# Layer 0 of a two-layer attention trunk: the rotation summed in PSUM, the heads' combination moved from VectorE to GpSimd

## The chip, the core and the metric

The kernel runs on one core of a Trainium2 chip. The metric is the device time of one execution in microseconds (us). The engines are named as the profile names them: PE is TensorE (matmuls; PEld its weight loads), DVE is VectorE, ACT is ScalarE, POOL is GpSimd, SP is SyncE, which issues the DMAs here. Each engine takes its own instructions in the order in which they stand; semaphores let one wait for another. SBUF is the memory that all of them work in; PSUM holds the results of matmuls, in eight banks of 128 partitions x 512 float32. The time before is a median of 2046.3 us over three runs (2044.1 to 2049.32).

## The reference

Two layers over 1024 tokens of width 1024, each a normalisation, a mixer and a residual. Layer 0 mixes with dilated window attention: 16 heads of 64, each in three groups with (window, dilation) = (128, 1), (512, 4), (2048, 16), so 48 attentions, whose results are combined by their softmax denominators and gated. Cut to what matters here:

```python
def dilated_mixer(h, w_in, w_out):
    proj = h @ w_in
    q = rope(qkv[:, :, 0], pos)          # x1*cos - x2*sin, x2*cos + x1*sin
    k = rope(qkv[:, :, 1], pos)
    v = qkv[:, :, 2]
    for g, (window, dil) in enumerate(DIL_GROUPS):
        o, lse = dilated_window_attention(q[:, :, sl], k[:, :, sl], v[:, :, sl], window, dil)
        ...
    alpha = jax.nn.softmax(jnp.stack(lses, axis=0), axis=0)
    o = jnp.sum(alpha[..., None] * jnp.stack(outs, axis=0), axis=0)
    y = o.reshape(B, S, DIL_WIDTH) * jax.nn.silu(gate)
    return y @ w_out
```

Layer 1 is a differential attention of eight heads. All of it is float32. The kernel splits each matrix operand into a high part that the matmul takes whole and a low part (the rest), and adds three products, so that a float32 product costs three matmuls.

## The kernel before, in words

The transposed, normalised input stays in SBUF as `XH` (high) and `XL` (low). First come the values of layer 0 and most of its gates. Then two strands run interwoven on PE. One is the attention: 8 pairs of heads x 3 groups x 2 heads, each head in four steps `c` of two blocks of 128 queries: `scores` (with the masked minimum on DVE at L583 and the exponential on ACT at L586), three steps later `transposes` (PE at L599; ACT casts the high part `pp`, L603, and DVE subtracts it from PSUM to get the low part, L122), and five steps later `product` with the values. The other strand, the filler, makes the rotated queries and keys in 24 units, one for a pair and a group (`qk_unit`).

A unit loads two weight blocks of 128 x 1024 (`raw`), splits each into `wh` (ACT, L184) and `wl` (`low`, L122), and runs for each half of the tokens (512) two projections of 24 matmuls, one for each half of the head dimension, into two PSUM tiles `pp[0]` and `pp[1]`. Both have the tag `pj` of the pool `ps`. That pool has four tags of two buffers of one bank (`pj`, `s`, `pt`, `u`), so that the next projection takes the bank of `pp[0]` again. On the engines, the tiles of the projections are called `pqk`. The rotation (L247 to L252) makes four products on DVE from `pp` and the tables into SBUF tiles `t`, and the difference and the sum on POOL into `r`; in groups 1 and 2 the output of these is put in the order of the residues (`put`, strided). Then `r` is split again (ACT L256, `low` alternating between DVE and POOL by `alt()`) and stored to DRAM, from which the heads load it.

`product` ends with the sum of the high and the low half of the values, into `u`: for groups 0 and 1 in `store` (L654 on ACT copies one half from PSUM to the single buffer `ul`, L659 on DVE adds), for group 2 in `alone` (L645 and L647 on ACT, L646 and L649 on DVE, the last one from SBUF to SBUF, strided). When the third group of a pair has its scores, `put_stats` and `joint` send the softmax statistics through DRAM (`st_d` to `js`, some small operations on DVE from L691 on, then `wt_d`), and after its last product `combine` loads the weights as `wb`, multiplies the three `u` (L715), adds them (L720), multiplies with the gate (L721), and `put_y` splits and stores the result.

PE's order is written out by hand: it is the order of the program. A filler step is taken wherever `fill.at` is called, three times in each step of the attention, up to a goal that grows by four matmuls a call; before the attention it runs 2.4 units ahead (`LEAD0`). The order on the other engines is chosen by a scheduler when the program is built.

Of the kernel before, what the change touches and what calls it, by code (L numbers as in the profile page):

```python
# [10 lines left out]
F32 = mybir.dt.float32  # L11
F32R = mybir.dt.float32r
# [80 lines left out]
def trunk(ctx: ExitStack, tc: tile.TileContext, a: dict, out: bass.AP):  # L93
# [126 lines left out]
    def qk_unit(pool, unit, w, sub=1, on_pool=False):  # L220

        tiles = []
        for half in range(2):
            wh, wl = w_tiles([P, KT, P])
            split(wh, wl, load(w[half], [P, KT, P]))
            tiles.append((wh, wl))
        r = [pool.tile([P, T], F32, tag="r", name="r", bufs=3 - on_pool) for _ in range(2)]
        for c in range(2):
            tok = ts(c, 512)
            pp = []  # L230
            for half in range(2):
                o = ps.tile([P, 512], F32, tag="pj", name="pqk")
                yield from project(o, *tiles[half], tok)
                pp.append(o)
            nat = (lambda t: t) if sub == 1 else (lambda t: t.rearrange("p (a r) -> p a r", r=sub))
            put = lambda t: t.rearrange("p (r c a) -> p c a r", r=sub, c=2)[:, c]
            if sub == 1:
                put = lambda t: t[:, tok]
            x, eng = pp, nc.vector
            if on_pool:  # L240
                x, eng = [pool.tile([P, 512], F32, tag="x", name="x") for _ in range(2)], nc.gpsimd
                for i in range(2):
                    nc.scalar.copy(x[i], pp[i])
            t1, t2, t3, t4 = (
                pool.tile([P, 512], F32, tag="t", name="t", bufs=3 - on_pool) if i < 2 or not on_pool
                else x[i - 2] for i in range(4))
            eng.tensor_mul(t1, x[0], cos[:, tok])  # L247
            eng.tensor_mul(t3, x[0], sin[:, tok])
            eng.tensor_mul(t2, x[1], sin[:, tok])  # L249
            nc.gpsimd.tensor_sub(put(r[0]), nat(t1), nat(t2))  # L250
            eng.tensor_mul(t4, x[1], cos[:, tok])  # L251
            nc.gpsimd.tensor_add(put(r[1]), nat(t4), nat(t3))  # L252
        written.add(unit)
        for e in range(2):
            rh = pool.tile([P, T], F32R, tag="rh", name="rh")
            nc.scalar.copy(rh, r[e])  # L256
            low(nc.vector if on_pool else alt(), r[e].bitcast(F32R), r[e], rh)
            for i, t in enumerate((rh.bitcast(F32), r[e])):
                nc.sync.dma_start(qk_d[unit, :, :, i, e].rearrange("s h f t -> f (s h) t"), t)
# [99 lines left out]
    def put_y(layer, kt, c, y, hi):  # L359
# [7 lines left out]
        nc.scalar.copy(hi, y)  # L367
        low(nc.vector, y.bitcast(F32R), y, hi)
# [160 lines left out]
    with tc.tile_pool(name="l0", bufs=2) as lp, early0 as ep:  # L529
# [4 lines left out]
        class Head:  # L534
# [99 lines left out]
            def alone(self, c):  # L634
# [14 lines left out]
                nc.vector.tensor_add(by_residue(uo, SUB[2])[:, 2 * c : 2 * c + 2, :], us_[:HD], ul)  # L649
# [56 lines left out]
        def combine(pr, us):  # L706
            fill.until(("gate", 0, pr))
            for c in range(2):
                tok = ts(c, 512)
                for g in range(NG):  # L710
# [4 lines left out]
                    (nc.vector if pr == 7 else alt()).tensor_mul(us[g][:, tok], us[g][:, tok], wb)  # L715
                sil = lp.tile([P, 512], F32, tag="sil_in", name="sil_in", bufs=1)
                nc.sync.dma_start(sil, sil_d[0][pr, :, tok])
                y = us[0][:, tok]
                for g in (1, 2):
                    (nc.vector if pr == 7 else nc.gpsimd).tensor_add(y, y, us[g][:, tok])  # L720
                nc.vector.tensor_mul(y, y, sil)  # L721
                put_y(0, pr, c, y, us[1][:, tok])
# [20 lines left out]
        for i in range(nst + LAG_P):  # L743
            if i < nst:
                hd, c = heads[i // 4], i % 4
                if c == 0 and hd.h == 0:
                    stats[hd.pr, hd.g] = lp.tile([P, 2, 2, NB], F32, tag="st", name="st")
                    us[hd.pr, hd.g] = lp.tile([P, T], F32, tag="u", name="u", bufs=3)
# [322 lines left out]
```

## Time and profile before

| | us |
|---|---|
| median of three runs | 2046.3 |
| the profiled execution, its own time | 2049.16 |
| its span, first to last instruction | 2047.3 |
| PE busy (share of the span) | 1911.4 (93%) |
| DVE busy | 1145.4 (56%) |
| ACT busy | 886.6 (43%) |
| POOL busy | 617.5 (30%) |

The profile is of one execution. In its groups, a row gives line, engine, operation and tiles (output<-inputs), their number, the busy time, the mean of one in ns, and after the bar the idle time of the engine just before and what ended it. A row of the timeline gives start, duration, engine, line, operation, and in brackets the idle time before and what ended it. Lines named L122, L184 are in the helpers `low` and `split` and serve many places; the tile names tell which. Matmuls overlap, so the duration of one is longer than the distance to the next. A row of the windows gives, for a stretch, the busy time of each engine (number of instructions), the granted share of the TensorE clock, the DMA engines' busy share and GB/s.

### The profile page before, as it was taken

To read this page: it belongs to the slowest core of one execution; us is meant where nothing else is said; L and a number is where in the kernel's file an instruction comes from. 1 tells how busy PE (TensorE), PEld (TensorE's weight loads), DVE (VectorE), ACT (ScalarE), POOL (GpSimd) and SP (SyncE) were. 2 spreads that over 40 slices of the span, in tenths; PEclk is the share of its full clock that TensorE was granted. 3 is DMA by queue.
4 is the path that set the end of the run, shared out by engine and by line. 5 is a ranking of instruction groups with operands and counts; after the bars stand their busy time and mean duration, and the time that the engine had idled before them with its cause. 6 is when DMAs were issued, how large, how long until landed. Compare 5 with 4: busy or idle time off the path is not lost.

```text
span 2047.3 us, 28864 instructions
## 1 busy us (share of the span) xinstructions
PE 1911.4 (93%) x10008; PEld 1598.6 (78%) x10008; DVE 1145.4 (56%) x2771; ACT 886.6 (43%) x2055; POOL 617.5 (30%) x386
## 2 busy tenths in 40 slices
PE   6999999999999999999999969899999899999888
PEld 4788888888787787788787848688879788887776
DVE  3311122146776767676767655570066877777626
ACT  3312122135555555555555555341245455546522
POOL 2000000143443434353535330230561534433121
PEclk8999999999999999999999979899999999999999
DMA  5424244277696969696969697542446565555643
GB/s 207 145 93 138 99 146 161 102 222 231 198 298 192 296 190 304 182 301 191 299 197 297 195 328 227 183 172 97 142 154 190 165 196 162 195 183 177 239 155 124
DMA packets 218018, 397.90 MB, mean 194 GB/s; under 512 B 40976, under 2 KB 123408, under 8 KB 217872
## 3 DMA queue, kind: packets, MB, share of 16 engines
q1 hardware_dynamic: 217872, 396.04, 60.7%
q8 instruction: 80, 1.31, 0.3%
q14 instruction: 66, 0.54, 0.1%
HBM read 254.87 MB, written 132.71 MB: 189 GB/s over the span
## 4 chain that ended last, share of the span: by engine, by line
PE 67%; DVE 11%; DMA 10%; ACT 4%; POOL 3%; issue 3%; SPq 1%; POOLq 0%; DVEq 0%; ACTq 0%
PE pqk L275 25%; PE pv L213 16%; PE pg L275 7%; PE po L377 3%; PE sc L576 3%; DMA wb<-wt_d 2%; PE sc L894 2%; PE up L626 2%; PE pe L420 2%; PE tp L599 2%; PE ob L945 2%; DVE u L649 1%; DMA st_d<-st 1%; POOL r L252 1%; DVE pm L897 1%
## 5 line engine op out<-in xcount | busy, mean ns | idle before, releaser
L275 PE MATMUL pqk<-XL,wh 128*128 128x512 f32 x1024 | 423.1, 413 | 0.0
L275 PE MATMUL pqk<-XH,wl 128*128 128x512 f32 x1024 | 411.8, 402 | 0.0
L275 PE MATMUL pqk<-XH,wh 128*128 128x512 f32 x1024 | 410.7, 401 | 0.9 <-DVE t L251 0.9
L122 POOL TENSOR_TENSOR wl<-raw,wh 128x1024 fp32r<-128x1024 f32 x41 | 98.5, 2402 | 612.1 <-ACT wh L184 612.1
L586 ACT ACTIVATE pm<-pm,st 128x128 f32<-128x128 f32 (+1 forms) x384 | 170.2, 444 | 155.9 <-DVE st L583 154.0
L275 PEld LDWEIGHTS pqk<-XH,wh 128*128 128x128 f32 x1024 | 194.9, 190 | 30.4 <-DVE t L251 1.9
L275 PEld LDWEIGHTS pqk<-XL,wh 128*128 128x128 f32 x1024 | 195.3, 191 | 27.6
L275 PEld LDWEIGHTS pqk<-XH,wl 128*128 128x128 f32 x1024 | 195.6, 191 | 27.2
L213 PE MATMUL pv<-vwh,XH 128*128 128x512 f32 (+1 forms) x448 | 173.8, 388 | 8.3 <-ACT XH L158 4.6
L250 POOL TENSOR_TENSOR r<-t 128x512 f32<-128x512 f32 x64 | 98.1, 1533 | 270.2 <-DVE t L249 269.2
L213 PE MATMUL pv<-vwl,XH 128*128 128x512 f32 (+1 forms) x448 | 172.4, 385 | 2.8 <-POOL vwl L122 2.8
L213 PE MATMUL pv<-vwh,XL 128*128 128x512 f32 (+1 forms) x448 | 172.6, 385 | 1.4 <-DVE XL L122 0.8
L184 ACT CAST wh<-raw 128x1024 fp32r<-128x1024 f32 x98 | 102.5, 1047 | 151.6 <-PE pqk L275 73.3
L122 DVE TENSOR_TENSOR wl<-raw,wh 128x1024 fp32r<-128x1024 f32 x57 | 76.0, 1333 | 147.6 <-ACT wh L184 147.3
L122 DVE TENSOR_TENSOR vs<-pv,vs 128x512 fp32r<-128x512 f32 x64 | 44.1, 689 | 200.5 <-ACT vs L495 187.9
L904 ACT ACTIVATE pm<-pm,mx 128x256 f32<-128x256 f32 (+7 forms) x128 | 99.4, 777 | 123.2 <-DVE mx L903 64.8
L122 DVE TENSOR_TENSOR pp<-tp,pp 128x512 fp32r<-128x512 f32 (+2 forms) x192 | 104.0, 541 | 80.8 <-ACT pp L603 79.2
L599 PE MATMUL tp<-ident,pm 128*128 128x128 f32 x560 | 96.3, 281 | 39.8 <-DVE pp L122 39.5
L599 PEld LDWEIGHTS tp<-ident,pm 128*128 128x128 f32 x560 | 73.1, 144 | 73.1 <-issue 36.5
L583 DVE CUSTOM_DVE_ANT_0 pm<-sc,masks 128x128 f32<-128x128 f32 (+1 forms) x384 | 118.7, 343 | 17.1 <-PE sc L576 15.7
L897 DVE CUSTOM_DVE_ANT_0 pm<-sc,md 128x512 f32<-128x512 f32 (+3 forms) x192 | 102.7, 551 | 31.1 <-PE sc L894 28.6
L495 ACT CAST vs<-pv 128x512 fp32r<-128x512 f32 x48 | 28.1, 586 | 187.2 <-PE pv L213 187.2
(516 smaller groups left out, 4441.0 us busy)
## 6 DMA issues: line engine op xcount, KB each, us to landing
qk_d<-rh SPq DMA_DIRECT2D x64, 512.0 KB
qk_d<-r SPq DMA_DIRECT2D x64, 512.0 KB
qh<-qk_d SPq DMA_DIRECT2D x128, 256.0 KB
ql<-qk_d SPq DMA_DIRECT2D x128, 256.0 KB
ka<-qk_d SPq DMA_DIRECT2D x64, 512.0 KB
v_d<-vs SPq DMA_DIRECT2D x48, 512.0 KB
raw<-in_dil_qk_dram SPq DMA_DIRECT2D x48, 512.0 KB
vt<-v_d SPq DMA_DIRECT2D x48, 512.0 KB
```

The lines of the kernel that those rows point to most:

```text
L122: eng.tensor_tensor(o, full, hi.bitcast(F32), ALU.subtract)
L184: nc.scalar.copy(wh, raw)
L213: nc.tensor.matmul(o, lhsT=l, rhs=r_, start=first and k == 0, stop=last and k == 3 * KT - 1, skip_group_check=True)
L250: nc.gpsimd.tensor_sub(put(r[0]), nat(t1), nat(t2))
L275: nc.tensor.matmul(o, lhsT=l[:, kt, :], rhs=r_[:, kt, tok], start=k == 0, stop=k == 3 * KT - 1)
L377: nc.tensor.matmul(banks[c], lhsT=l[:, kt, ts(n)], rhs=r_[:, ts(c, 512)], start=first and k == 0, stop=last and k == 2,)
L576: nc.tensor.matmul(sc[:, cols], lhsT=q[:, ts(b)], rhs=kv, start=k == 0, stop=k == 1)
L583: nc.vector.tensor_tensor_reduce(pm[:, cols], sc[:, cols], m[:, m.shape[1] - w_ :], 1.0, 3.0e38, ALU.add, ALU.min, st[:, 0, j : j + 1])
L586: nc.scalar.activation(pm[:, cols], pm[:, cols], AF.Exp, bias=st[:, 0, j : j + 1], scale=-1.0, accum_out=st[:, 1, j : j + 1])
L599: nc.tensor.transpose(out=tp[:, ts(n)], in_=self.pb.pop((b, kb)), identity=ident)
L897: nc.vector.tensor_tensor_reduce(pm[:, k0:k1], sc[:, :w_], m_, 1.0, 3.0e38, ALU.add, ALU.min, mx[:, j : j + 1])
L904: nc.scalar.activation(pm[:, :wq], pm[:, :wq], AF.Exp, bias=mx[:, 0:1], scale=-1.0, accum_out=den)
```

## The change

- `qk_unit` in layer 0 makes the whole rotation on DVE. The product of `pp[1]` and the sines is written into `pp[0]`, the product of `pp[1]` and the cosines into `pp[1]` itself, and the difference and the sum are taken by DVE, each from one SBUF tile and one PSUM tile. The four `t` tiles become two.
- Both weight splits and both low parts of `r` are done by POOL (before, half of them).
- In `alone`, the last sum (from `us_` and `ul` into `u`) is done by POOL.
- `combine` runs on POOL for the pairs 0 to 6 (for pair 7 on DVE, as before), in the group order 0, 2, 1, with each sum right after its product; the gate and the high and low parts of `put_y` are done by the same engine. The gate's tile shares the three buffers of `wb`. `u` has four buffers, not three.

Layer 1 keeps its rotation on POOL.

```diff
@@ def qk_unit
-            split(wh, wl, load(w[half], [P, KT, P]))
+            split(wh, wl, load(w[half], [P, KT, P]), None if on_pool else nc.gpsimd)
...
-            t1, t2, t3, t4 = (
-                pool.tile([P, 512], F32, tag="t", name="t", bufs=3 - on_pool) if i < 2 or not on_pool
-                else x[i - 2] for i in range(4))
-            eng.tensor_mul(t1, x[0], cos[:, tok])
-            eng.tensor_mul(t3, x[0], sin[:, tok])
-            eng.tensor_mul(t2, x[1], sin[:, tok])
-            nc.gpsimd.tensor_sub(put(r[0]), nat(t1), nat(t2))
-            eng.tensor_mul(t4, x[1], cos[:, tok])
-            nc.gpsimd.tensor_add(put(r[1]), nat(t4), nat(t3))
...
+                t1, t2 = (pool.tile([P, 512], F32, tag="t", name="t") for _ in range(2))
+                nc.vector.tensor_mul(t1, pp[0], cos[:, tok])
+                nc.vector.tensor_mul(t2, pp[0], sin[:, tok])
+                nc.vector.tensor_mul(pp[0], pp[1], sin[:, tok])
+                nc.vector.tensor_sub(put(r[0]), nat(t1), nat(pp[0]))
+                nc.vector.tensor_mul(pp[1], pp[1], cos[:, tok])
+                nc.vector.tensor_add(put(r[1]), nat(pp[1]), nat(t2))
...
-            low(nc.vector if on_pool else alt(), r[e].bitcast(F32R), r[e], rh)
+            low(nc.vector if on_pool else nc.gpsimd, r[e].bitcast(F32R), r[e], rh)
@@ def put_y(layer, kt, c, y, hi, eng=None)
-        nc.scalar.copy(hi, y)
-        low(nc.vector, y.bitcast(F32R), y, hi)
+        if eng is None:
+            nc.scalar.copy(hi, y)
+        else:
+            eng.tensor_copy(hi, y)
+        low(eng or nc.vector, y.bitcast(F32R), y, hi)
@@ def alone
-                nc.vector.tensor_add(by_residue(uo, SUB[2])[:, 2 * c : 2 * c + 2, :], us_[:HD], ul)
+                nc.gpsimd.tensor_add(by_residue(uo, SUB[2])[:, 2 * c : 2 * c + 2, :], us_[:HD], ul)
@@ def combine
+            eng = nc.vector if pr == 7 else nc.gpsimd
             for c in range(2):
                 tok = ts(c, 512)
-                for g in range(NG):
+                y = us[2][:, tok]
+                for g in (0, 2, 1):
...
-                    (nc.vector if pr == 7 else alt()).tensor_mul(us[g][:, tok], us[g][:, tok], wb)
-                sil = lp.tile([P, 512], F32, tag="sil_in", name="sil_in", bufs=1)
+                    eng.tensor_mul(us[g][:, tok], us[g][:, tok], wb)
+                    if g:
+                        eng.tensor_add(y, y, us[1 if g == 1 else 0][:, tok])
+                sil = lp.tile([P, 512], F32, tag="wb", name="sil_in", bufs=3)
                 nc.sync.dma_start(sil, sil_d[0][pr, :, tok])
-                y = us[0][:, tok]
-                for g in (1, 2):
-                    (nc.vector if pr == 7 else nc.gpsimd).tensor_add(y, y, us[g][:, tok])
-                nc.vector.tensor_mul(y, y, sil)
-                put_y(0, pr, c, y, us[1][:, tok])
+                eng.tensor_mul(y, y, sil)
+                put_y(0, pr, c, y, us[1][:, tok], eng)
@@ the loop of layer 0
-                    us[hd.pr, hd.g] = lp.tile([P, T], F32, tag="u", name="u", bufs=3)
+                    us[hd.pr, hd.g] = lp.tile([P, T], F32, tag="u", name="u", bufs=4)
```

The scheduler's new order, at three places. In these rows a name in brackets is the engine or DMA queue whose semaphore the instruction waits for; ISA is the masked minimum. Line numbers of the changed kernel are its own: L253 to L258 are the rotation, L592 the minimum, L655 and L658 the sums of `alone`, L700 the first operation of `joint`, L727 the product with the weights.

DVE at the first unit's first half of the tokens, before the attention starts. Before:

```order
L247 TENSOR_TENSOR t<-pqk,cos 128x512 [waits DMAHW5_49,DMAHW4_49,DMAHW6_49,DVE_49,PE_49]
L248 TENSOR_TENSOR t<-pqk,sin 128x512
L249 TENSOR_TENSOR t<-pqk,sin 128x512 [waits PE_49]
L251 TENSOR_TENSOR t<-pqk,cos 128x512 [waits Pool_49]
L247 TENSOR_TENSOR t<-pqk,cos 128x512 [waits DVE_49,PE_49]
```

And in the changed kernel:

```order
L253 TENSOR_TENSOR t<-pqk,cos 128x512 [waits DMAHW5_49,DMAHW4_49,DMAHW6_49,DVE_49,PE_49]
L254 TENSOR_TENSOR t<-pqk,sin 128x512
L255 TENSOR_TENSOR pqk<-pqk,sin 128x512 [waits DVE_49,PE_49]
L257 TENSOR_TENSOR pqk<-pqk,cos 128x512
L256 TENSOR_TENSOR r<-t,pqk 128x512 [waits DVE_49]
L258 TENSOR_TENSOR r<-pqk,t 128x512 [waits DVE_49]
L253 TENSOR_TENSOR t<-pqk,cos 128x512 [waits DVE_49,PE_49]
```

The last reader of `pp[0]` is now the subtraction L256, fourth behind the wait for `pp[1]`'s first reader L255 and its neighbour L257; before, it was L248, ahead of that wait.

DVE at the change from pair 0 to pair 1, where the filler works on the unit of pair 1, group 2. Before:

```order
L249 TENSOR_TENSOR t<-pqk,sin 128x512 [waits PE_49]
L122 TENSOR_TENSOR pp<-tp,pp 128x256 [waits Activation_49]
L646 TENSOR_TENSOR us__3681<-us__3681,up 128x256 [waits Activation_49]
L583 ISA pm,st<-sc,masks 128x256 [waits PE_49]
L583 ISA st 128x1
L583 ISA pm,st<-sc,masks 128x256
L583 ISA st 128x1
L691 TENSOR_TENSOR jm<-js 128x16 [waits DMAHW6_49,DMAHW4_49]
L649 TENSOR_TENSOR u<-us__3681,ul 64x2x128 [waits Activation_49]
L251 TENSOR_TENSOR t<-pqk,cos 128x512 [waits Pool_49]
```

And in the changed kernel:

```order
L255 TENSOR_TENSOR pqk<-pqk,sin 128x512 [waits DVE_49,PE_49]
L257 TENSOR_TENSOR pqk<-pqk,cos 128x512
L122 TENSOR_TENSOR pp<-tp,pp 128x256 [waits DVE_49,Activation_49]
L655 TENSOR_TENSOR us__3661<-us__3661,up 128x256 [waits Activation_49,Pool_49]
L700 TENSOR_TENSOR jm<-js 128x16 [waits DMAHW5_49,DMAHW3_49]
L256 TENSOR_TENSOR r<-t,pqk 128x64x8 [waits DMAHW4_49,DVE_49]
L258 TENSOR_TENSOR r<-pqk,t 128x64x8 [waits DMAHW2_49,DVE_49]
L701 TENSOR_TENSOR jm<-jm,js 128x16 [waits DVE_49]
```

The operation that waits for the statistics' DMA stands ahead of the subtraction. The same order, L255, others, L700, L256, stands at each of the seven changes of pair; at the other places inside the attention, one `pp` or none, and once a `store` sum of 64x2x256 or 64x512, stands between L257 and L256.

The combination of pair 0: before, one of its products on DVE, with the low part of a transposed block behind it:

```order
L649 TENSOR_TENSOR u<-us__3776,ul 64x2x128 [waits Activation_49]
L715 TENSOR_TENSOR u<-u,wb 128x512 [waits DMAHW2_49,DMAHW1_49]
L122 TENSOR_TENSOR pp<-tp,pp 128x512 [waits Activation_49]
L646 TENSOR_TENSOR us__3816<-us__3816,up 128x256 [waits Activation_49]
L583 ISA pm,st<-sc,masks 128x128 [waits PE_49]
```

In the changed kernel, on POOL:

```order
L658 TENSOR_TENSOR u<-us__3717,ul 64x2x128 [waits Activation_49]
L727 TENSOR_TENSOR u<-u,wb 128x512 [waits DMAHW7_49,DMAHW1_49,Pool_49]
L122 TENSOR_TENSOR wl<-raw,wh 128x1024 [waits DMAHW4_49,PE_49,Activation_49]
L727 TENSOR_TENSOR u<-u,wb 128x512 [waits DMAHW4_49,DMAHW3_49]
L658 TENSOR_TENSOR u<-us__3754,ul 64x2x128 [waits Activation_49,Pool_49]
L658 TENSOR_TENSOR u<-us__3794,ul 64x2x128 [waits DVE_49,Activation_49]
L122 TENSOR_TENSOR wl<-raw,wh 128x1024 [waits PE_49,Activation_49,Pool_49]
```

The products with the weights, the splits and the sums of group 2 now stand in one queue, POOL's.

13 lines of the change are left out of this document (10 added, 3 removed).

## The prediction

> **What bounds the kernel now.** I read the page's busy times first, then the stretch from 435 to 1175 us, which holds the attention of layer 0 without its ends, then who TensorE (PE) waited for there, then the timelines of the two places where the change acts.
>
> ```profile
> PE 1911.4 (93%) x10008; PEld 1598.6 (78%) x10008; DVE 1145.4 (56%) x2771; ACT 886.6 (43%) x2055; POOL 617.5 (30%) x386
> 435.00:1175.00 740.00, 704.95 (x3881) 595.57 (x3880) 522.39 (x1370) 401.92 (x1127) 313.59 (x173) 0.98 0.78 239
> PE tp L599 <- DVE pp L122: 39.5, 18, 5.6
> PE pqk L275 <- DVE t L251: 0.9, 2, 0.7
> ```
>
> PE sets the end: in those 740 us it is busy 705, DVE 522, ACT 402, POOL 314 (columns: stretch, length, PE, PEld, DVE, ACT, POOL, granted clock, DMA share, GB/s). Its waits from 435 to 1200 us are few: 39.5 us in 18 waits for DVE's low part of a transposed block, and 0.9 us at the projections. So two things count: those waits, which the change can remove, and any new wait of PE. The waits lie where a pair of heads ends:
>
> ```profile
> 553.75 0.69 DVE L715 TENSOR_TENSOR u<-u,wb 128x512 f32<-128x512 f32 x1 [2.48 <-DMA wb<-wt_d]
> 555.10 0.66 PE L599 MATMUL tp<-ident,pm 128*128 128x128 f32 x4 [2.14 <-DVE pp L122]
> 567.90 2.89 DVE L715 TENSOR_TENSOR u<-u,wb 128x512 f32<-128x512 f32 x1
> 568.13 0.96 PE L599 MATMUL tp<-ident,pm 128*128 128x128 f32 x4 [3.21 <-DVE pp L122]
> 770.04 0.88 PE L599 MATMUL tp<-ident,pm 128*128 128x128 f32 x3 [2.34 <-DVE pp L122]
> 555.10:558.50 3.40, 3.40 (x21) 3.05 (x22) 2.89 (x8) 3.06 (x8) 3.13 (x3) 1.00 0.46 142
> 568.30:571.70 3.40, 3.40 (x13) 3.01 (x13) 3.40 (x3) 0.95 (x2) 3.40 (x2) 0.50 0.98 378
> 769.70:773.10 3.40, 3.06 (x11) 2.71 (x12) 3.40 (x5) 2.69 (x6) 2.25 (x3) 0.50 1.03 246
> ```
>
> DVE stands 2.48 us at the combination, waiting for the weights' DMA, with the transposes' low part queued behind, and where POOL works at the same time its product of two SBUF tiles takes 2.89 us instead of 0.69. The last rows show a second price. After an idle PE of 2.14 us the clock stayed at 1.00, after 2.34 and 3.21 us it was 0.50 for 3.4 us. At 0.50 such a stretch issued 13 matmuls; at 1.00 the next quoted row gives 59 in 10 us, or 20 in 3.4 us. So it costs about 7/20 of 3.4 us, 1.2 us.
>
> ```profile
> 690.00:700.00 10.00, 10.00 (x59) 8.61 (x58) 6.63 (x20) 5.53 (x15) 4.06 (x2) 1.00 0.86 235
> ```
>
> **What is removed.** POOL takes the combination for seven of eight pairs and the last sums of group 2, and `us` has a fourth buffer, so DVE no longer stands at the weights. I take all 39.5 us as gone. The mean clock of 0.98 over 740 us is some 30 us at 0.50, nine stretches of 1.2 us: 11 us more. Together 50 us, the most that this part can give; if POOL, now in the same place, hands the wait on, it is less.
>
> **What is added: PE's wait for its own bank.** Each unit makes four projections of 24 matmuls in the two banks of tag `pj`. Before, the first bank was read by L247 and L248 while the second filled, so the next projection found it free:
>
> ```profile
> 402.00 0.69 DVE L247 TENSOR_TENSOR t<-pqk,cos 128x512 f32<-128x512 f32 x1 [2.67 <-PE pqk L275]
> 402.61 0.68 DVE L248 TENSOR_TENSOR t<-pqk,sin 128x512 f32<-128x512 f32 x1
> 407.17 0.39 PE L275 MATMUL pqk<-XH,wl 128*128 128x512 f32 x1
> 407.40 0.40 PE L275 MATMUL pqk<-XH,wh 128*128 128x512 f32 x1
> 407.60 0.69 DVE L249 TENSOR_TENSOR t<-pqk,sin 128x512 f32<-128x512 f32 x1 [4.31 <-PE pqk L275]
> 535.18 0.39 PE L275 MATMUL pqk<-XH,wl 128*128 128x512 f32 x1
> 535.41 0.39 PE L275 MATMUL pqk<-XH,wh 128*128 128x512 f32 x1
> ```
>
> The matmul at 407.17 is the last of a second half; the next projection starts at 407.40, in the first bank, before L249 has even begun. Now the product of the second half and the sines is written into that first bank and read again by the subtraction. The bank is therefore free only after two dependent DVE operations that cannot start before the second half is complete. Nothing stands on PE between the two projections: the filler hands out four matmuls at a time, and with its lead of 231 matmuls (2.4 units of 96, rounded up) matmul 240, 288 and so on are the first of their four. The rows at 535 us, inside the attention, show the same neighbours. So there are 24 units x 2 = 48 such places, and PE waits at each.
>
> The price of one, from rows: DVE starts at 407.60, 0.20 us after PE would have gone on. A 512-wide operation lets the next one start after 0.61 us (402.00 to 402.61). DVE's order puts the cosine product (L257) ahead of the subtraction, so 0.61 + 0.61, then the subtraction itself, then some 0.1 us to PE (the `pp` that freed 568.13 ended at 567.99, below). The subtraction takes 0.69 us in group 0. In groups 1 and 2 its output is strided, and a strided 512-wide sum took 1.08:
>
> ```profile
> 523.47 1.08 DVE L659 TENSOR_TENSOR u<-up,ul 64x512 f32<-64x512 f32 x1
> 524.59 0.69 DVE L251 TENSOR_TENSOR t<-pqk,cos 128x512 f32<-128x512 f32 x1
> 465.37 0.68 DVE L659 TENSOR_TENSOR u<-up,ul 64x512 f32<-64x512 f32 x1
> 465.98 0.54 DVE L122 TENSOR_TENSOR pp<-tp,pp 128x384 fp32r<-128x384 f32 x1
> 466.44 0.40 DVE L583 CUSTOM_DVE_ANT_0 pm<-sc,masks 128x256 f32<-128x256 f32 x1
> 526.33 0.42 DVE L122 TENSOR_TENSOR pp<-tp,pp 128x256 fp32r<-128x256 f32 x1
> 526.66 0.28 DVE L583 CUSTOM_DVE_ANT_0 pm<-sc,masks 128x128 f32<-128x128 f32 x1
> 567.30 0.69 DVE L122 TENSOR_TENSOR pp<-tp,pp 128x512 fp32r<-128x512 f32 x1
> 529.51 2.13 DVE L649 TENSOR_TENSOR u<-us__3543,ul 64x256 f32<-64x256 f32 x1 [0.59 <-ACT ul L647]
> 541.23 0.17 DVE L691 TENSOR_TENSOR jm<-js 128x16 f32<-128x16 f32 x1 [2.86 <-DMA js<-st_d]
> ```
>
> That is 2.2 us bare and 2.6 us strided. No row has DVE writing PSUM: not below 0.42 us (a `pp` half as wide), not above 1.08; I take 0.69, since reading PSUM or SBUF makes no difference in these rows. Inside the attention the order adds, ahead of the subtraction, a `pp` (0.61, 0.47 or 0.34 us for 512, 384 or 256 wide), once a store of `u` (1.1, strided), and at each change of pair the first step of the joint softmax. That one waits for the statistics' way through DRAM: at 541.23, while PE passed the place at 535.41. From 541.23 on, 0.1 + 1.08 + 0.1 makes 7.1 us; DVE loses the sum of 2.13 us ahead of the last statistics, so they may come earlier by 1.5 us; bounds 4 and 7.1, and I take 6. By the six places of a pair: 2.8, 2.2, 4.2, 2.9, 6.0, 2.6, which is 20.7; seven pairs give 145. The six halves of the first three units have no neighbours but L257: 2 x 2.2 + 4 x 2.6 = 15. Together **160 us**; bounds: 48 x 2.2 = 106 and, with 7.1 us at each change and 1 us more of queue at the 28 places with neighbours, 196.
>
> **Clock.** 39 of the 48 waits are 2.6 us or longer by this count, that is 2.4 or more as the profile counts idle time, just above the 2.34 that halved the clock. Three in four of them at 1.2 us: **35 us**, bounds 17 (only the two long ones of each of seven pairs) and 47.
>
> The Trainium skill, "TensorE: Matmul & The Clock Gate", section "HAM oscillation — how this bites in real kernels", puts the limit at PE gaps over some 3.4 us. Here 2.34 us was enough, so the row decides; by the Trainium skill's limit only the two long waits of a pair would count, the 17 us above.
>
> **The rest, off PE's path.** POOL loses the rotation's sums and gains, per pair, six splits and six low parts of 2.4 us, sixteen operations of the combination of about 1.6 and eight sums of group 2 of about 0.7: 60 us of a pair that lasts some 122 (104 from 568.13 to the same wait of the next pair, at 671.98, and an eighth of 160 + 35 - 50). DVE loses more than it gains (its half of the splits and low parts, the combination, the sums against 12 operations of 0.69 or 1.08 per pair).
>
> ```profile
> L122 POOL TENSOR_TENSOR wl<-raw,wh 128x1024 fp32r<-128x1024 f32 x22 | 52.8, 2399 | 81.3 <-ACT wh L184 81.3
> L122 POOL TENSOR_TENSOR r<-r,rh 128x1024 fp32r<-128x1024 f32 x22 | 52.7, 2394 | 18.6 <-ACT rh L256 17.4 <-DMA vt<-v_d 1.2
> L720 POOL TENSOR_TENSOR u<-u 128x512 f32<-128x512 f32 x24 | 39.9, 1673 | 1.2 <-DMA wb<-wt_d 0.7
> POOL u L715 <- DMA wb<-wt_d: 22.1, 9, 5.1
> 671.98 0.45 PE L599 MATMUL tp<-ident,pm 128*128 128x128 f32 x1 [3.21 <-DVE pp L122]
> ```
>
> The cover of these edits is half a unit (104/6, 17 us) between a split and its first matmul. ACT loses 14 casts and no longer finds `ul` free until POOL has added it, and there is one buffer: the point of the fourth rival. The last pair stays on DVE, layer 1 is unchanged: 0.
>
> **The sum.** 2049.16 (the profiled execution) - 50 + 160 + 35 = 2194 us. That execution is 2.9 us over the median of 2046.3, so I say **2190 us**.
>
> **Rivals.**
> 1. Faster: the waits at the banks are hidden and the 50 us remain, 1999 us. It decides where a wait is under 50/48 = 1.04 us; for it, DVE is idle 4.31 us ahead of L249. Against it: PE is busy without a gap there, no other bank is left (four tags of two fill the eight), and even the subtraction put directly behind the sine product needs 0.20 + 0.61 + 0.69. Chance 0.04; no change, where by accident both cancel, 0.01.
> 2. The bare wait only, neighbours long done and no clock lost: 106 - 50, **2105 us**. For it: DVE gets idle time while PE waits. Against it: the order is fixed, and the joint step waits for a DMA. 0.15.
> 3. Short gaps leave the clock at full, only the two long waits of a pair lose it: 17 instead of 35, **2176 us**. For it: each wait stands alone, 17 us from the next; the gaps that lost the clock came with others. Against it: 2.34 us at 770. 0.15. The Trainium skill's limit ("TensorE: Matmul & The Clock Gate") would have it so.
> 4. POOL becomes what PE waits for at the change of pair: the weights' wait, 2.4 us splits and low parts stand ahead of group 2's sums, ACT stands at `ul`, and `pp` behind it: two waits of 4 us in seven pairs, and the clock each time: 56 + 17, **2267 us**. For it: POOL stood 5.1 us at one `wb` before. Against it: PE, held 6 us at the same change, gives the weights time to land. 0.13.
>
> The forecast keeps 0.52 (its own range 2150 to 2225). The range, **2110 to 2250**, leaves out half of rival 2, most of rival 4 and the fast side. Faster by over 0.3% (what a measurement here can tell): 0.04; within 0.3%: 0.01; slower: 0.95.
>
> **What would show it.** In the profile after: PE's projections waiting for DVE's subtraction, some 48 times and 130 to 190 us in all; the longest, about 6 us, seven times, at the joint step; the 39.5 us at the transposes nearly gone; the clock of this stage at 0.95 or less; DVE's busy time down, POOL's up by about 100 us (60 us a pair against its 314 of 740 us, 44 a pair, before). Wrong would be: no wait at the projections (then rival 1), waits of 2 us each at full clock (2), or waits of ACT or PE that end with POOL (4).

## The result, and the profile after

The changed kernel takes **2196.5 us** (median of four runs, 2193.59 to 2201.63), against 2046.9 for the kernel before on the same chip: the ratio is 1.073, with a 95% interval of 1.071 to 1.076. The forecast was 2190, with a range of 2110 to 2250. The profiled execution took 2193.59 us, 144.4 more than the one of before.

From the page of the changed kernel, its busy times:

```profile
PE 1973.4 (90%) x10008; PEld 1643.7 (75%) x10008; DVE 1057.8 (48%) x2706; ACT 887.5 (40%) x2041; POOL 678.8 (31%) x465
```

From its windows, the stretch that holds the attention of layer 0, now longer (columns as before: stretch, length, PE, PEld, DVE, ACT, POOL, clock, DMA share, GB/s):

```profile
435.00:1300.00 865.00, 743.43 (x3751) 620.48 (x3752) 437.55 (x1266) 391.25 (x1071) 351.52 (x230) 0.91 0.67 200
```

And from its waits, what TensorE (PE) stood at in the attention (us in total, times, the longest):

```profile
PE pqk L281 <- DVE r L256: 131.6, 47, 4.4
PE pg L281 <- DVE r L256: 5.3, 1, 5.3
PE tp L608 <- DVE pp L122: 0.4, 1, 0.4
```

VectorE (DVE) has 88 us less to do than before, and it is the engine PE now waits for. PE waits 48 times, 136.9 us in all, for the subtraction that frees the first bank of the projections. The 39.5 us at the transposes have become 0.4. The clock of the stage fell from 0.98 to 0.91.

One such wait, inside the first pair. From the timeline of the changed kernel, first DVE, then PE (start, duration, engine, line, operation; in brackets the idle time before and what ended it):

```profile
509.55 0.70 DVE L255 TENSOR_TENSOR pqk<-pqk,sin 128x512 f32<-128x512 f32 x1 [2.23 <-PE pqk L281]
510.15 0.69 DVE L257 TENSOR_TENSOR pqk<-pqk,cos 128x512 f32<-128x512 f32 x1
510.75 0.68 DVE L256 TENSOR_TENSOR r<-t,pqk 128x512 f32<-128x512 f32 x1
511.35 0.55 DVE L122 TENSOR_TENSOR pp<-tp,pp 128x384 fp32r<-128x384 f32 x1
...
509.07 0.44 PE L281 MATMUL pqk<-XH,wl 128*128 128x512 f32 x1
511.48 0.79 PE L281 MATMUL pqk<-XH,wh 128*128 128x512 f32 x1 [1.98 <-DVE r L256]
```

The matmul at 509.07 completes the second half; the next projection would have followed 0.23 us later. DVE was idle and began at once. Its three operations in a row, 0.60 us apart, are all that PE waits for: 2.19 us from 509.30 to 511.48. The pair change, where the subtraction stands behind the wait for the statistics, in the same two views:

```profile
571.06 0.70 DVE L255 TENSOR_TENSOR pqk<-pqk,sin 128x512 f32<-128x512 f32 x1 [1.90 <-PE pqk L281]
571.67 0.69 DVE L257 TENSOR_TENSOR pqk<-pqk,cos 128x512 f32<-128x512 f32 x1
572.27 0.41 DVE L122 TENSOR_TENSOR pp<-tp,pp 128x256 fp32r<-128x256 f32 x1
572.60 0.41 DVE L655 TENSOR_TENSOR us__3661<-us__3661,up 128x256 f32<-128x256 f32 x1
573.34 0.18 DVE L700 TENSOR_TENSOR jm<-js 128x16 f32<-128x16 f32 x1 [0.34 <-DMA js<-st_d]
573.44 1.03 DVE L256 TENSOR_TENSOR r<-t,pqk 128x512 f32<-128x512 f32 x1
...
570.63 0.40 PE L281 MATMUL pqk<-XH,wl 128*128 128x512 f32 x1
574.52 0.50 PE L281 MATMUL pqk<-XH,wh 128*128 128x512 f32 x1 [3.50 <-DVE r L256]
```

The DMA costs DVE only 0.34 us here; the operations ahead of it cost more. The hold, counted from where PE would have gone on, is 3.66 us.

The clock, from the windows of the changed kernel: up to the end of the first of these waits, the 3.5 us behind it, and the 3.5 us behind the wait of the pair change.

```profile
507.00:511.40 4.40, 2.51 (x15) 1.89 (x13) 2.17 (x6) 3.00 (x7) 1.38 (x1) 1.00 1.09 288
511.40:514.90 3.50, 3.42 (x10) 2.94 (x11) 2.52 (x8) 2.53 (x5) 3.26 (x2) 0.51 0.99 212
574.50:578.00 3.50, 3.48 (x19) 2.95 (x20) 3.00 (x16) 1.34 (x5) 0.00 (x0) 1.00 0.30 92
```

A wait of 1.98 us halved the clock; one of 3.50 us did not (the last section shows why). In the whole attention the trace has 37 stretches at 0.50, 167 us long together, against 7 of 27 us before. By the matmuls issued in them they cost some 64 us, against 11 before; this is an estimate.

What the other queues stood at, from the waits of the changed kernel (POOL is GpSimd, ACT ScalarE):

```profile
DVE jm L700 <- DMA js<-st_d: 3.6, 6, 1.2
POOL u L727 <- DMA wb<-wt_d: 42.3, 16, 9.6
ACT ul L663 <- POOL u L658: 17.5, 6, 3.7
```

DVE hardly stands at the statistics. POOL does stand at the weights and ACT at POOL's sums, but no wait of PE in the attention ends with either.

### The profile page after: what moved, and what is told of

Same layout as the page of the kernel before. It is cut to its first block, busy times and chain, and to the rows that moved or that the text cites. A ratio compares the mean times of both kernels' runs of the same rounds, so it can differ in the third digit from the quotient of the medians.

```text
span 2191.9 us, 29066 instructions
## 1 busy us (share of the span) xinstructions
PE 1973.4 (90%) x10008; PEld 1643.7 (75%) x10008; DVE 1057.8 (48%) x2706; ACT 887.5 (40%) x2041; POOL 678.8 (31%) x465
## 4 chain that ended last, share of the span: by engine, by line
PE 74%; DVE 11%; DMA 7%; issue 3%; ACT 2%; POOL 2%; SPq 1%; DVEq 0%; POOLq 0%; ACTq 0%
PE pqk L281 31%; PE pv L213 14%; PE pg L281 7%; PE sc L585 4%; PE po L386 3%; PE tp L608 3%; PE pe L429 3%; PE up L635 2%; PE sc L905 2%; DMA st_d<-st 2%; DVE r L256 2%; PE ob L956 2%; DVE pqk L257 1%; DVE pm L908 1%; PE tp L936 1%
## 5 line engine op out<-in xcount | busy, mean ns | idle before, releaser
L281 PE MATMUL pqk<-XH,wh 128*128 128x512 f32 x1024 | 435.5, 425 | 131.6 <-DVE r L256 131.6
L281 PE MATMUL pqk<-XL,wh 128*128 128x512 f32 x1024 | 440.8, 430 | 0.0
L281 PE MATMUL pqk<-XH,wl 128*128 128x512 f32 x1024 | 426.5, 417 | 0.0
L122 POOL TENSOR_TENSOR wl<-raw,wh 128x1024 fp32r<-128x1024 f32 x65 | 155.9, 2399 | 863.7 <-ACT wh L184 852.8
L281 PEld LDWEIGHTS pqk<-XH,wh 128*128 128x128 f32 x1024 | 206.5, 202 | 177.8 <-DVE r L256 141.6
L612 ACT CAST pp<-tp 128x512 fp32r<-128x512 f32 (+2 forms) x192 | 90.0, 469 | 140.4 <-PE up L635 95.2
L592 DVE CUSTOM_DVE_ANT_0 pm<-sc,masks 128x128 f32<-128x128 f32 (+1 forms) x384 | 119.5, 347 | 56.5 <-PE sc L585 53.7
L122 POOL TENSOR_TENSOR r<-r,rh 128x1024 fp32r<-128x1024 f32 x48 | 113.7, 2392 | 21.7 <-ACT rh L262 21.3
L122 DVE TENSOR_TENSOR wl<-raw,wh 128x1024 fp32r<-128x1024 f32 x33 | 44.3, 1341 | 140.9 <-ACT wh L184 140.7
L585 PE MATMUL sc<-ka,ql 128*128 128x128 f32 (+1 forms) x384 | 110.3, 299 | 0.0
L281 PE MATMUL pg<-XH,wh 128*128 128x512 f32 x256 | 102.6, 401 | 5.3 <-DVE r L256 5.3
```

What stands on the lines that cost most here:

```text
L122: eng.tensor_tensor(o, full, hi.bitcast(F32), ALU.subtract)
L281: nc.tensor.matmul(o, lhsT=l[:, kt, :], rhs=r_[:, kt, tok], start=k == 0, stop=k == 3 * KT - 1)
L585: nc.tensor.matmul(sc[:, cols], lhsT=q[:, ts(b)], rhs=kv, start=k == 0, stop=k == 1)
L592: nc.vector.tensor_tensor_reduce(pm[:, cols], sc[:, cols], m[:, m.shape[1] - w_ :], 1.0, 3.0e38, ALU.add, ALU.min, st[:, 0, j : j + 1])
L612: nc.scalar.copy(pp[:, 0, :w_], tp[:, :w_])
```

## The experiments

The comparisons are with the kernel before, timed on the same chip, as medians and as a ratio with its 95% interval. `sr` and `js` have one buffer each, not two, in the kernels that need room in SBUF for more tiles `t`, or for a fourth `u` beside them.

**The sine product in SBUF.** The bank stays free of DVE's products; all else is the changed kernel.

```diff
-                t1, t2 = (pool.tile([P, 512], F32, tag="t", name="t") for _ in range(2))
+                t1, t2, t3 = (pool.tile([P, 512], F32, tag="t", name="t", bufs=3) for _ in range(3))
...
-                nc.vector.tensor_mul(pp[0], pp[1], sin[:, tok])
-                nc.vector.tensor_sub(put(r[0]), nat(t1), nat(pp[0]))
+                nc.vector.tensor_mul(t3, pp[1], sin[:, tok])
+                nc.vector.tensor_sub(put(r[0]), nat(t1), nat(t3))
```

> The changed kernel, with the product of the second half and the sines written to a third SBUF tile t instead of into pp[0] (two small tiles of joint and put_stats get one buffer to make room); all else as changed. Theory (PE waits for its own bank): the 137 us of waits of PE for DVE's subtraction go to under 5 us and the clock in the attention goes back to 0.97 or more, so 2196 - 145 - 50 to 60, that is 1990 to 2005 us. Rival (POOL's queue or DVE's sums set the pace once the banks do not): PE waits at the transposes or at the weights' low parts by 40 us or more, and the time is 2040 us or more.

Measured: 1999.3 us (1996.75 to 2006.26), ratio 0.976 (0.973 to 0.979). From its windows and its waits:

```profile
435.00:1175.00 740.00, 719.09 (x4015) 608.69 (x4015) 486.78 (x1370) 415.91 (x1170) 394.25 (x257) 0.99 0.87 258
```

```profile
PE tp L608 <- DVE pp L122: 5.6, 7, 2.2
PE pe L429 <- DMA XH<-y_d: 13.1, 4, 8.7
```

No wait for a bank of the projections, no stretch at half clock in the attention until its last pair (from 1140 us on), and 49 us less than the 2048.4 of before beside it. So the place of one temporary is worth 197 us; the 137 us of waits and the 64 us of clock make 201. The rest of the change takes these 49 us off, but not all of them where it acts. The profiled executions are 52 us apart: 45 of it lie in the attention (from the first projection to the last transposed statistics, `tps`), 4 come back right behind it, and 11 are in layer 1, whose code is the same. Layer 1 lasted 673.8 us in that execution of the kernel before, 663.2 here, and 665.6 to 670.2 in the twelve others. The repair has a price that the path doesn't feel. From the groups of this kernel, and then of the changed one:

```profile
L256 DVE TENSOR_TENSOR r<-t 128x512 f32<-128x512 f32 x48 | 73.9, 1539 | 0.0
```

```profile
L256 DVE TENSOR_TENSOR r<-t,pqk 128x512 f32<-128x512 f32 x48 | 43.8, 912 | 0.0
```

With both inputs in SBUF the subtraction takes 1.54 us in the mean, with one in PSUM 0.91; the last section takes these means apart.

**The rotation as before, the rest changed.**

```diff
-                nc.vector.tensor_mul(pp[0], pp[1], sin[:, tok])
-                nc.vector.tensor_sub(put(r[0]), nat(t1), nat(pp[0]))
-                nc.vector.tensor_mul(pp[1], pp[1], cos[:, tok])
-                nc.vector.tensor_add(put(r[1]), nat(pp[1]), nat(t2))
+                nc.vector.tensor_mul(t2, pp[1], sin[:, tok])
+                nc.gpsimd.tensor_sub(put(r[0]), nat(t1), nat(t2))
+                nc.vector.tensor_mul(t4, pp[1], cos[:, tok])
+                nc.gpsimd.tensor_add(put(r[1]), nat(t4), nat(t3))
```

> The changed kernel with the rotation as before (four products into SBUF tiles t, difference and sum on POOL), so that the rest of the change stands alone: splits and low parts on POOL, sum of group 2 and combination on POOL, fourth buffer of u. Theory: no wait at the banks; the 39.5 us at the transposes and 11 us of clock go, 1995 to 2010 us, if POOL (20 us a pair more than in the changed kernel, 80 of some 97) keeps up. Rival: POOL does not, and PE waits for low parts or transposes: 2030 us or more.

Measured: 2011.4 us (2008.05 to 2011.52), ratio 0.981 (0.979 to 0.984), just above the range of the theory. The waits of 137 us are gone here too. From its waits, what is new:

```profile
PE pqk L281 <- DVE t L257: 10.1, 6, 2.4
```

And from its groups, the product that PE waits for, with what DVE waited for ahead of it:

```profile
L257 DVE TENSOR_TENSOR t<-pqk,cos 128x512 f32<-128x512 f32 x48 | 33.0, 687 | 49.9 <-POOL r L256 49.4
```

POOL, which now also has the rotation's sums (busy 802.1 us, 40%), frees the tiles `t` late, DVE reads PSUM late for it, and PE waits a little for that.

**The rotation alone**, on the kernel before (splits, low parts, sums and the combination stay where they were): the `+` lines of the rotation in the change's diff, nothing else.

> The kernel before with the rotation of the changed kernel alone (products into PSUM, difference and sum on DVE); splits, low parts, sums and combination as before. Theory: 48 waits at the banks of 2.2 us or more as in the changed kernel, and the 39.5 us at the transposes stay or shrink by what PE's waits give DVE: 2046 + 145 + 40 to 60, less 0 to 40: 2190 to 2250 us. Rival (the loss is in the moves to POOL): under 2120 us.

Measured: 2268.1 us (2265.34 to 2272.38), ratio 1.107 (1.104 to 1.110). From its waits and its windows:

```profile
PE pqk L281 <- DVE r L256: 178.8, 47, 9.0
PE pg L281 <- DVE r L256: 7.5, 1, 7.5
```

```profile
435.00:1175.00 740.00, 606.93 (x3001) 506.22 (x3000) 449.32 (x1117) 316.24 (x859) 131.93 (x70) 0.89 0.62 185
```

The loss is all in this part, and more than expected: with the combination still on it, DVE has more ahead of the subtraction, the longest waits are 6 to 9 us, and the clock falls to 0.89. The rest of the change, which gives 49 us when nothing holds the bank, gives 72 here.

**One matmul more in the lead.** The fours of the filler then end where a half ends, so that a piece of the attention stands between the two projections.

```diff
-LEAD0, LATE0 = 2.4, 1
+LEAD0, LATE0 = 232 / 96, 1
```

> The changed kernel with the filler's lead at 232 instead of 231 matmuls, so that the last matmul of a second half is the last of its four, and the scores of the next step (four matmuls, some 0.45 us) stand between it and the next projection. Theory: each of the 44 waits inside the attention is shorter by 0.4 to 0.5 us, 18 to 22 us together, and the shortest no longer halve the clock, 0 to 25 us: 2150 to 2178 us. Rival (the waits are not the cause, or other work on DVE slides into the gap): within 6 us of 2196.

Measured: 2133.8 us (2126.43 to 2136.79), ratio 1.041 (1.038 to 1.044), below what was expected. From its waits:

```profile
PE pqk L281 <- DVE r L256: 101.6, 47, 4.6
```

The waits fall by 33 us, and the half clock costs 33 us in place of 64: many holds are now 1.7 to 2.1 us. The order on DVE, which is chosen anew, may be part of it; this run can't tell the two apart.

**Without the neighbour.** The cosine product goes to `t1`, which the subtraction reads, so it can't stand ahead of it.

```diff
-                nc.vector.tensor_mul(pp[1], pp[1], cos[:, tok])
-                nc.vector.tensor_add(put(r[1]), nat(pp[1]), nat(t2))
+                nc.vector.tensor_mul(t1, pp[1], cos[:, tok])
+                nc.vector.tensor_add(put(r[1]), nat(t1), nat(t2))
```

> The changed kernel, with the product of the second half and the cosines written over t1 instead of into pp[1], so that it cannot stand ahead of the difference that reads t1; the difference still reads the product in pp[0]. In DVE's order L257 leaves the place between L255 and L256, all else there stays. Theory (the wait is the count of DVE operations up to the difference): 0.61 us less at the places with other neighbours, 0.5 at the others, some 27 us of 137; the gaps are then 1.6 to 3.9 us and fewer halve the clock, 15 to 35 us more: 2135 to 2155 us. Rival (the wait is set by something else, as the PSUM writes or the statistics' DMA): within 10 us of 2196.

Measured: 2165.1 us (2161.21 to 2171.34), ratio 1.057 (1.055 to 1.060). From its waits, and DVE's and PE's timeline at the first pair change:

```profile
PE pqk L281 <- DVE r L256: 84.6, 40, 3.2
PE pqk L281 <- DVE jm L701: 35.9, 7, 6.2
```

```profile
565.27 0.70 DVE L255 TENSOR_TENSOR pqk<-pqk,sin 128x512 f32<-128x512 f32 x1 [1.89 <-PE pqk L281]
569.56 0.18 DVE L700 TENSOR_TENSOR jm<-js 128x16 f32<-128x16 f32 x1 [2.94 <-DMA js<-st_d]
569.65 1.01 DVE L256 TENSOR_TENSOR r<-t,pqk 128x512 f32<-128x512 f32 x1
570.51 0.16 DVE L701 TENSOR_TENSOR jm<-jm,js 128x16 f32<-128x16 f32 x1
...
570.72 0.79 PE L281 MATMUL pqk<-XH,wh 128*128 128x512 f32 x1 [5.48 <-DVE jm L701]
```

One instruction less between the product and the subtraction takes 31 us off, 13 of waits (123.8 are left) and 17 of clock (47 are left). It is less than expected since the pair change gives back: PE arrives there earlier, while the statistics land by their own way, and DVE stands 2.94 us at them where it stood 0.34 (21.3 us in eight waits in place of 7.1). (The seven waits that the profile puts down to L701 are for the subtraction as well: the two end within 0.01 us of each other, at 570.66.)

**What the combination gives.** The kernel with the sine product in SBUF, and in it the combination as before (`put_y` too), with three buffers of `u`:

```diff
-            eng = nc.vector if pr == 7 else nc.gpsimd
...
-                    eng.tensor_mul(us[g][:, tok], us[g][:, tok], wb)
+                    (nc.vector if pr == 7 else alt()).tensor_mul(us[g][:, tok], us[g][:, tok], wb)
...
-                    us[hd.pr, hd.g] = lp.tile([P, T], F32, tag="u", name="u", bufs=4)
+                    us[hd.pr, hd.g] = lp.tile([P, T], F32, tag="u", name="u", bufs=3)
```

> The kernel with the sine product in SBUF (e1), with the combination of the kernel before (products alternating between DVE and POOL, gate and low part on DVE, high part on ACT, three buffers of u); splits, low parts and the sum of group 2 stay on POOL. Theory (DVE's standing at the weights' DMA made the waits at the transposes): they come back, 25 to 45 us and 5 to 15 us of clock: 2030 to 2055 us. Rival (the gain came from the splits, low parts and the sum of group 2 leaving DVE): 1995 to 2015 us.

Measured: 2020.1 us (2019.14 to 2024.3), ratio 0.987 (0.985 to 0.988), between the two ranges. From its waits:

```profile
PE tp L608 <- DVE pp L122: 7.2, 6, 2.1
PE up L635 <- issue: 11.0, 1, 11.0
```

The theory's cause falls: DVE stands at the weights again (19.7 us in 13 waits), yet PE's waits at the transposes stay at 7.2 us. Half of the 21 us over 1999.3 is one wait of PE at the last change of pair, of the kind that the next run has at all seven.

The same kernel with the last line of that diff alone, so the combination on POOL over three buffers:

> The kernel with the sine product in SBUF (e1), with three buffers of u instead of four, all else on POOL as there. Theory (the fourth buffer lets the next pair's first group be stored while POOL combines): DVE stands at the first store of the next pair until POOL has read the old u, and PE behind it, 1 to 10 us at each of seven changes: 2005 to 2070 us. Rival (the buffer is free in time): within 5 us of 1999.

Measured: 2046.4 us (2040.23 to 2052.8), ratio 0.999 (0.997 to 1.000). From its waits, and from the timelines of POOL, DVE and PE at one of them:

```profile
PE up L635 <- issue: 42.9, 7, 14.4
```

```profile
576.58 1.26 POOL L729 TENSOR_TENSOR u<-u 128x512 f32<-128x512 f32 x1
577.87 0.68 DVE L668 TENSOR_TENSOR u<-up,ul 64x512 f32<-64x512 f32 x1 [1.78 <-POOL u L729]
578.66 0.66 PE L635 MATMUL up<-pp,vt 128*128 128x256 f32 x2 [5.13 <-issue]
```

With three buffers the combination on POOL gives nothing over the kernel before, and takes back the 47 us: the next pair's first store on DVE (L668) waits for the last reader of the old `u`, POOL's sum (L729), and the products on PE (L635) wait for the store to free their bank.

And the kernel before with the combination on POOL and the fourth buffer, all else as it was: the lines of `put_y`, `combine` and of the loop of layer 0 in the change's diff.

> The kernel before with one part of the change alone: the groups' combination on POOL over four buffers of u; rotation, splits, low parts and group 2's last sum stay where they were (one buffer each of the two side tiles makes the room). Theory (this part makes the whole gain that the change has once its rotation doesn't hold the bank): 1990 to 2010, and the waits of PE for the normalized values at the transposes, 39.5 us before, under 10 us. Rival (it needs the rotation off POOL too, since POOL would carry both): 2025 to 2050.

Measured: 2036.3 us (2027.89 to 2041.33), ratio 0.993 (0.991 to 0.995). From its waits:

```profile
PE tp L608 <- DVE pp L122: 12.9, 13, 2.0
PE pqk L281 <- DVE t L257: 12.5, 9, 2.3
```

The theory falls; the time lies in the rival's range. Against the kernel before on the same chip, the combination alone gives 13 us, the other parts without it 29 (with the bank free), both 49. In the attention alone, by the profiled executions, it is 22, 18 and 45; the combination then loses 5 behind it, where PE waits 12.7 us for the last results (`XH` from `y_d`), 3.3 before. The waits at the transposes fall from 39.5 to 12.9, but as in the kernel with the rotation as before, PE waits for the rotation's readers, since POOL carries its sums and the combination.

**Two pieces moved back to DVE**, in the kernel with the sine product in SBUF: group 2's last sum (the first line); then, apart from it, the splits and low parts, alternating as before (the other two); then both.

```diff
+                nc.vector.tensor_add(by_residue(uo, SUB[2])[:, 2 * c : 2 * c + 2, :], us_[:HD], ul)
...
+            split(wh, wl, load(w[half], [P, KT, P]))
...
+            low(nc.vector if on_pool else alt(), r[e].bitcast(F32R), r[e], rh)
```

> The kernel with the sine product in SBUF (e1), with the last sum of group 2 back on DVE, as before the change. In e1 DVE waited 46.6 us for ul behind ACT, which finds ul free only when POOL has added. Theory (that sum on POOL costs nothing on PE's path, and on DVE it stood at most 2.1 us beside POOL's work): PE's waits at the transposes grow a little or not, 1990 to 2010 us. Rival (taking that sum from DVE is what freed the transposes): 2020 to 2045 us.

> The kernel with the sine product in SBUF (e1), with the splits of the weights and the low parts of r alternating between DVE and POOL, as before the change. Theory (the gain of e1 over the kernel before is the combination and the fourth buffer, together, not the splits): within 10 us of 1999. Rival (DVE's products of two SBUF tiles held the transposes): 2015 to 2045 us.

> The kernel with a third tile for the product with the sine, with two more moves undone at once: the splits and low parts alternate between DVE and POOL as in the kernel before, and DVE makes group 2's last sum. Theory (each of the two took 5 to 6 us off by itself, from 1999.3 to 1993.8 and 1993.4; what they leave of the 5.6 us of waits at the transposes is the same wait for the normalized values, so they don't add up fully): 1988 to 1995. Rival (they take off different waits and add up): 1984 to 1988. Rival (DVE, which gets both back, becomes late for the projections): above 1997.

Measured: 1993.4 us (1992.28 to 1995.96), ratio 0.972 (0.969 to 0.974); 1993.8 us (1992.09 to 1995.91), 0.972 (0.970 to 0.975); both 2008.3 us (2004.37 to 2009.08), 0.980 (0.976 to 0.983). From the waits of the last:

```profile
PE tp L608 <- DVE pp L122: 16.5, 13, 2.6
```

Each alone may be 5 to 9 us better than leaving both on POOL (the intervals just overlap); both together are not. DVE's busy time from 435 to 1175 us goes from 487 (none) to 536 and 517 (one) to 573 (both), and with the last the transposes wait for it again; so the last rival's time came (above 1997), though it put the wait at the projections, where there is none. The two with one piece are the fastest kernels here, 2.8% below the kernel before.

**The pair before the last on DVE**, for the 13.1 us at the end of the attention where PE waits for the last results to come back through DRAM.

```diff
-            eng = nc.vector if pr == 7 else nc.gpsimd
+            eng = nc.vector if pr >= 6 else nc.gpsimd
```

> The kernel with the sine product in SBUF (e1), and the combination of pair 6 on DVE as that of pair 7. PE waited 13.1 us for XH from y_d at the end of layer 0 there, 2.8 in the changed kernel, and I take it that pair 6's result comes late from POOL. Theory: 5 to 9 us less than 1999. Rival (the wait is for the loads themselves, or DVE holds the transposes at that place): no change or up to 8 us more.

Measured: 2005.0 us (2004.19 to 2007.82), ratio 0.979 (0.978 to 0.981). From its waits:

```profile
PE pe L429 <- DMA XH<-y_d: 13.9, 4, 9.7
```

Unchanged: the theory falls, and the time is within the rival's range. What holds the last transfer stays open. In the kernel with the sine product in SBUF the DMA engines' share is 1.04 from 1150 to 1175 us, where PE waits, against 0.87 in the attention, so the loads themselves are the nearer reading; no run tests it.

## Why the prediction was right, and where not

**What bounds the kernel: right.** PE sets the end, and its waits and its clock give the time.

**The 50 us removed: right in size, in part by luck.** The 39.5 us fell to 0.4 in the changed kernel, and the kernel with the sine product in SBUF stands at the 1999 us that the first rival worked out for 50 us with no new wait. But by the profiled executions only some 41 of these 50 come from layer 0 (45 in the attention, less 4 behind it); that layer 1 was 11 us shorter than in the one of before is luck. The term was also incomplete in its cause, DVE at the weights: the combination alone gives 13, the other parts alone 29 with DVE at the weights as before, and without the fourth buffer POOL does hand a wait on, as the term's last sentence allowed.

**PE's wait for its own bank: right, to 14 us.** Forecast 48 waits and 160 us; the distances in the timeline give 48 and 146. By place:

| place in a pair | forecast | in the first pairs, repeated in the later |
|---|---|---|
| first three units, six halves | 2.2 to 2.6 | 2.14 to 2.96 |
| 1, 2 | 2.8, 2.2 | 2.79, 2.19 |
| 3, 4 | 4.2, 2.9 | 3.89, 2.87 |
| 5, the pair change | 6 | 3.5 to 4.5, mean 3.9 |
| 6 | 2.6 | 2.50 |

The last pair differs: 3.99 us at place 4, and 5.47 at place 6, where a gate's projection comes next.

The term that was mis-sized is the pair change, "from 541.23 on ... bounds 4 and 7.1, and I take 6": seven times 2 us too much, which is the 14; the other places agree in sum. The statistics landed earlier, as seen from PE, than the 1.5 us allowed: DVE stood at L700 for 0.34 us at the first change and 3.6 in six waits together. Of the row that no trace had, DVE writing PSUM, the choice held: 0.70 us (L255), against 0.69 into SBUF. The strided difference took 1.03 for the 1.08 assumed.

**The clock: right in kind, too small.** Forecast 35 us added, measured 64. Two steps failed. There is no limit "just above the 2.34 that halved the clock": waits of 1.98 us halved it too, and one of 3.50 us did not. What counts is how much idle time falls into one window of a fixed grid, as the last section shows. The prediction's two rows fit this: its wait of 2.14 us lay across an edge of the grid, 1.67 us on one side and 0.47 on the other, and that of 2.34 us had 1.97 in one window. So there were 37 stretches, where three in four of 39 make 29. And a stretch is not always the 3.4 us assumed: 12 of the 37 last 6.8. The rate of 7/20 nearly held: of 167 us it makes 58. The third rival, that short gaps leave the clock, fell with this. The Trainium skill ("TensorE: Matmul & The Clock Gate", section "HAM oscillation — how this bites in real kernels") puts the limit at gaps over some 3.4 us; here that limit doesn't hold. The next section of that page, "A second HAM failure mode: psum-queue depth-cycling", is nearer: it tells of a kernel whose PE idles briefly between groups of matmuls as it goes round the PSUM banks, often enough that the clock falls again and again. The 37 stretches agree.

**The rest, off the path: right.** POOL's busy time rose by 61 us where 100 were named, and PE never waited for it; the fourth rival, POOL as the bound at the pair change, was not seen, though POOL stood 42.3 us at the weights. The second, the bare wait at full clock, failed by the clock and by the neighbours: 2.2 us x 48 is 106, and 146 were measured.

**The sum came out closer than its terms, by luck.** From the two profiled executions: 146 - 39 + 64 - 11 = 160, where 145 were forecast and 144.4 measured. The waits were 14 too high and the clock 29 too low; 12 us came back outside the attention: 4 behind it, and 8 in layer 1, whose code is the same and which was long in the execution of before. Another 2 came ahead of it (the first projection starts at 382.9 us, 385.0 before), and under 2 are not accounted for.

## What to carry to other kernels

Ask of each temporary who needs its memory next: a product written in place into a PSUM bank makes the bank's release wait for the instruction that writes it and for the one that reads it, and where two banks serve an engine that fills them without a pause, it pays that at every turn. Price such a wait by the instructions that stand ahead of the releasing one in its engine's order, the clock that short idles cost beside them (which can be forecast only as a share, since it depends on where each idle falls in the grid below), and the buffers; then look for the one tile in SBUF that undoes it. A part that loses can hide one that gains: taken apart, this change was 197 us of loss and 41 to 49 of gain.

## What the runs showed of the hardware

**The clock is decided by PE's idle time in windows of 3.41 us on a fixed grid, not by the length of one idle.** In the clock records of all fourteen kernels, every change of the clock lies on a grid of 3.41 us: of 586 changes none is off it by more than 0.004 us. Where the grid lies differs from execution to execution. The table adds up PE's idle time in each window of the grid, over the attention of all fourteen while the filler runs, for windows at full clock:

```
idle in the window, us     under 1.65   1.65 to 1.95   1.95 and more
windows                        2486            49            119
the next at half clock            0            26            119
```

The limit lies between, at about half of the window; the ends of matmuls in the trace are modelled, so it can't be read more finely. Outside that stretch six windows with 1.53 to 1.65 us of idle time were followed by one at half clock too, and there as well every one with 1.95 and more. It explains the two waits above. The window from 508.04 to 511.45 us had 1.94 us of idle time, nearly all of the wait of 1.98 us, and the next one was at half clock. The wait of 3.50 us was cut by the edge at 572.89 us into 1.87 and 1.63 us, and neither window had enough. It also explains the double stretches: a window at half clock was followed by another in 50 of the 52 cases with 0.5 us or more of idle time in it, and in none of 94 with under 0.25. The Trainium skill ("TensorE: Matmul & The Clock Gate", section "What's actually happening") says that the activity window is free-running; the grid agrees.

**An operand in PSUM spares DVE from POOL.** The means of 0.91 and 1.54 us above mix contiguous and strided subtractions, and those beside a busy POOL with those beside an idle one. Taken apart, from the timelines of the changed kernel and of the one with the sine product in SBUF (mean us of each, number in brackets; busy is POOL working for over half of the subtraction):

```
                               POOL idle     POOL busy
one input in PSUM, contiguous  0.68 (2)      0.68 (14)
one input in PSUM, strided     1.02 (12)     1.04 (19)
both in SBUF, contiguous       0.68 (2)      1.65 (14)
both in SBUF, strided          1.08 (11)     2.14 (14)
```

The Trainium skill ("SBUF — State Buffer", section "Who interferes with whom") has the rule: a DVE instruction with two SBUF inputs contends with a GpSimd instruction that reads SBUF, one with at most one such input doesn't. These rows agree.
